# A float32 decoder trunk with an S5 layer: four GLU weight blocks unsplit, the second scan ahead of the splits, and the S5 preparation in four column groups

## The chip, the cores and the metric

The kernel runs on one core of a Trainium2 chip. The metric is device time of one execution in microseconds (us), the median of several runs. PE is the matrix engine (TensorE), PEld its weight loads, DVE the vector engine, ACT the scalar engine, POOL GpSimd, SP the engine that issues the transfers.

## The reference

Two layers of a residual trunk over 256 positions of width 2048, all in float32. Layer 0 is stick-breaking attention beside gated linear attention; layer 1 is an S5 state-space mixer with a GLU. Each is followed by a SwiGLU network (inner width 5632). What the change touches is layer 1 (left out below: `bb` is B scaled by (lb - 1) / lam, and the states s follow from a scan over the positions, s at l = lb times s at l - 1, plus bu at l):

```python
def s5_mixer(h, lam_re, lam_im, log_step, b_re, b_im, c_re, c_im, d_skip, w_glu):
    u = h.reshape(b_, L, 128, 16)                      # 128 groups of 16 channels
    dt = jnp.exp(log_step)[:, None]
    mag, ang = jnp.exp(dt * lam_re), dt * lam_im       # 64 complex states a group
    lb_re, lb_im = mag * jnp.cos(ang), mag * jnp.sin(ang)
    ...
    bu_re = jnp.einsum('blgh,gph->blgp', u, bb_re)
    bu_im = jnp.einsum('blgh,gph->blgp', u, bb_im)
    ...
    y = (jnp.einsum('ghp,blgp->blgh', c_re, s_re)
         - jnp.einsum('ghp,blgp->blgh', c_im, s_im) + d_skip * u)
    y = jax.nn.gelu(y.reshape(b_, L, D_MODEL), approximate=False)
    val, gate = jnp.split(y @ w_glu, 2, axis=-1)       # w_glu: 2048 x 4096
    return val * jax.nn.sigmoid(gate)
```

## The kernel before

**Split products.** A large product is made of three cheap ones. `Stream` loads the weights in chunks of 512 rows by 512 columns (1 MB, three buffers `wraw`), in the order of a plan. `convert` splits half a chunk (a *unit*: 256 rows) into `whi`, rounded by ACT, and `wlo`, the rest, by DVE. The activations are split likewise into `xh` and `xl`. `products` (lines 190 to 192) then issues, for each 128 rows of weights and each half `tb` of the 256 positions, xh·whi, xh·wlo and xl·whi, so that a unit takes 12 matmuls of 512 columns. `linear` walks the units of one block of 512 output columns after the other. `pairwise` walks two blocks together, four units of rows at a time, and calls a hook ahead of a unit whose number is in its table.

**Background work.** `s5_prep` is a generator that `pump` advances between units while layer 0's SwiGLU network (`ffn(0, ...)`) runs. From the S5 parameters it makes tables on DVE and ACT, writes them to DRAM, reads them back, and multiplies them in small float32 products on PE (line 1221): for each of 16 `k`, two halves, each of 2 `ri` by 2 `q` matmuls with 32 output rows. They go to 32-column groups of the array, two groups in a half. A result is written out as `t_d`.

**Opening of layer 1.** The tail of the network's last block adds its output to the residual `h[0]` and `h[1]` (two halves of 128 positions; `close` updates four blocks of 512 columns of a half, `squares` sums their squares on ACT, `rstds` makes the reciprocal roots, `normed` scales). `hold` names the blocks of `h[0]` whose update is put off to the tail.

**S5 mixer (`layer1`).** The channels are in four groups G of four tiles. `stage_a` transposes the normed input (line 1374), `stage_v` and `stage_b` rearrange it into `U`, `stage_x` multiplies it by a table into `xt` (line 1398), `stage_t` transposes that (line 1407) and copies it into the state `X`. `scan(0)` covers G 0 and 1, `scan(1)` G 2 and 3: a `pairs(2)` over 15 chunks, 14 short steps that depend on one another, a `pairs(3)`, all on DVE; `steps(sc, n)` issues n of these 16. `within(G)` (line 1418) and `out(G)` (line 1470) form the output, which DVE transposes into `y` and ACT puts through Gelu. The first two GLU blocks are a `pairwise` of 16 units; the units 0 to 7 read G 0 and 1, the units 8 to 15 read G 2 and 3. `out(2)` and `out(3)` are issued by its hooks.

All engines run in the written order. Nearly all vector and scalar work is recorded at line 65, so that it is told apart by its tiles.

## Time and profile before

| | |
|---|---|
| median of 3 runs | 2222.76 us (2219.78 to 2223.53) |
| profiled execution | 2222.8 us |
| its span, first to last instruction | 2220.9 us |
| mean granted TensorE clock | 0.992 |
| PE busy | 2172.9 us, 98% of the span |
| DVE busy | 1380.1 us, 62% |
| ACT busy | 985.0 us, 44% |
| DMA | 457.44 MB, mean 206 GB/s |

The profile is of one execution. Its own time is 0.04 us above the median, and 1.9 us of it lie outside the span. Matmuls overlap at their ends, so that the distance between two starts, not the length of one, is what a matmul costs.

### The profile page before, as it was taken

The numbers are of one execution on the slowest core, as the hardware profiler recorded it, in microseconds if no ns is written. First come the engines' busy times: TensorE is split into PE (matmuls) and PEld (weight loads), VectorE is DVE, ScalarE is ACT, GpSimd is POOL, SyncE is SP. The second block draws the span as 40 slices with busy tenths as digits, with TensorE's granted clock in tenths as the row PEclk, the third lists the DMA queues.
The fourth block names the chain that finished last, engine by engine and source line by source line (L and its number), as shares of the span: only waits on it lengthen the run. The fifth ranks groups of instructions, "written<-read, shape, count | busy, mean of one in ns | idle before, by whom it ended". The sixth has DMA issues, their size and how long they took to land.

```text
span 2220.9 us, 27098 instructions
## 1 busy us (share of the span) xinstructions
PE 2172.9 (98%) x10704; PEld 1752.5 (79%) x10704; DVE 1380.1 (62%) x1917; ACT 985.0 (44%) x1242; POOL 7.1 (0%) x14
## 2 busy tenths in 40 slices
PE   8999999999999999999998699999999999999998
PEld 6888888788888887777776578878888888888886
DVE  4676645657779997895456875464544444444545
ACT  5444545464444444434344444464444444433433
POOL 0000000000000000000000000000000000000000
PEclk9999999999999999999999899999999999999999
DMA  7554554555687777898768846546555555555553
GB/s 228 170 180 153 166 174 152 190 193 174 224 250 245 236 238 243 275 284 264 242 203 330 334 155 212 182 171 208 174 190 180 196 178 197 175 193 186 189 171 133
DMA packets 266351, 457.44 MB, mean 206 GB/s; under 512 B 23248, under 2 KB 68576, under 8 KB 265328
## 3 DMA queue, kind: packets, MB, share of 16 engines
q1 hardware_dynamic: 265504, 451.00, 61.3%
q0 software_dynamic: 720, 4.72, 0.5%
q8 instruction: 84, 1.38, 0.2%
q14 instruction: 43, 0.35, 0.0%
HBM read 425.26 MB, written 30.41 MB: 205 GB/s over the span
## 4 chain that ended last, share of the span: by engine, by line
PE 94%; DVE 3%; ACT 1%; DMA 0%; issue 0%; SPq 0%; DVEq 0%; ACTq 0%
PE lin L190 30%; PE lin L192 29%; PE lin L191 29%; PE big L465 1%; PE big L1221 1%; DVE wlo L65 1%; DVE X L65 1%; PE big L192 0%; PE big L792 0%; PE big L191 0%; PE big L190 0%; DVE h L65 0%; DVE xl L65 0%; ACT xh L65 0%; DMA wraw<-w_in 0%
## 5 line engine op out<-in xcount | busy, mean ns | idle before, releaser
L65 DVE TENSOR_TENSOR wlo<-wraw,whi 128x1024 fp32r<-128x1024 f32 x713 | 864.8, 1234 | 563.4 <-ACT whi L65 563.0
L65 ACT CAST whi<-wraw 128x1024 fp32r<-128x1024 f32 x713 | 731.4, 1049 | 654.7 <-PE lin L192 578.1
L190 PE MATMUL lin<-whi,xh 128*128 128x512 f32 x2016 | 804.6, 399 | 11.0 <-ACT xh L65 11.0
L191 PE MATMUL lin<-wlo,xh 128*128 128x512 f32 x2016 | 798.1, 396 | 2.2 <-DVE wlo L65 2.1
L192 PE MATMUL lin<-whi,xl 128*128 128x512 f32 x2016 | 798.1, 396 | 1.2 <-DVE xl L65 1.2
L190 PEld LDWEIGHTS lin<-whi,xh 128*128 128x128 f32 x2016 | 380.8, 189 | 102.8 <-ACT xh L65 12.2
L192 PEld LDWEIGHTS lin<-whi,xl 128*128 128x128 f32 x2016 | 380.6, 189 | 92.5 <-DVE xl L65 3.7
L191 PEld LDWEIGHTS lin<-wlo,xh 128*128 128x128 f32 x2016 | 381.0, 189 | 91.5 <-DVE wlo L65 5.6
L190 PE MATMUL lin<-whi,ah 128*128 128x512 f32 x680 | 270.2, 397 | 0.0
L192 PE MATMUL lin<-whi,al 128*128 128x512 f32 x680 | 268.4, 395 | 0.0
L191 PE MATMUL lin<-wlo,ah 128*128 128x512 f32 x680 | 268.3, 394 | 0.0
L190 PEld LDWEIGHTS lin<-whi,ah 128*128 128x128 f32 x680 | 127.8, 188 | 32.2 <-issue 2.6
L192 PEld LDWEIGHTS lin<-whi,al 128*128 128x128 f32 x680 | 127.7, 188 | 30.7
L191 PEld LDWEIGHTS lin<-wlo,ah 128*128 128x128 f32 x680 | 127.8, 188 | 29.7
L65 DVE SCALAR_TENSOR_TENSOR a<-lin,rs,a 128x512 f32<-128x512 f32 x44 | 31.0, 747 | 60.0 <-PE lin L192 60.0
L65 ACT ACTIVATE a<-lin,rs 128x512 f32<-128x512 f32 x44 | 27.9, 684 | 90.0 <-PE lin L192 90.0
L65 ACT ACTIVATE junk<-yg 128x512 f32<-128x512 f32 x24 | 15.2, 632 | 74.2 <-DVE yg L65 74.2
L65 ACT CAST ah<-big 128x1024 fp32r<-128x1024 f32 x22 | 22.3, 1015 | 55.4 <-PE big L465 55.4
L65 DVE TENSOR_TENSOR ed<-C,lam 128x288 f32<-128x288 f32 x64 | 43.1, 673 | 4.4 <-DMA C<-s_c_re 4.4
L65 DVE TENSOR_TENSOR yg<-lin,yg 128x512 f32<-128x512 f32 x30 | 20.0, 689 | 41.3 <-PE lin L192 41.3
L65 DVE TENSOR_TENSOR tt<-C,lam 128x288 f32<-128x288 f32 x64 | 43.3, 676 | 0.5 <-DMA C<-s_c_im 0.5
L65 DVE TENSOR_TENSOR tt<-lam,B 128x256 f32<-128x256 f32 x56 | 37.5, 670 | 8.9 <-DMA win_d<-win 8.9
(316 smaller groups left out, 1273.3 us busy)
## 6 DMA issues: line engine op xcount, KB each, us to landing
wraw<-w_ffn_in SPq DMA_DIRECT2D x176, 1024.0 KB, 5.0
wraw<-w_ffn_out SPq DMA_DIRECT2D x88, 1024.0 KB, 5.3
wraw<-w_in SPq DMA_DIRECT2D x47, 1024.0 KB, 5.0
wraw<-w_glu SPq DMA_DIRECT2D x32, 1024.0 KB, 5.4
wraw<-w_out SPq DMA_DIRECT2D x16, 1024.0 KB, 5.0
e_d<-ed SPq DMA_DIRECT2D x64, 144.0 KB, 4.4
et<-e_d SPq DMA_DIRECT2D x32, 288.0 KB, 4.6
win_d<-win SPq DMA_DIRECT2D x32, 256.0 KB, 8.3
```

The source lines that it names most:

```text
L65: return f(*a, **k)
L190: mm(ps, lhsT=xh, rhs=hi[:, kk, :], start=(k == 0), stop=False)
L191: mm(ps, lhsT=xh, rhs=lo[:, kk, :], start=False, stop=False)
L192: mm(ps, lhsT=xl, rhs=hi[:, kk, :], start=False, stop=(k == len(acts) - 1))
L465: nc.tensor.transpose(p[:, tb, i, :], a[:, tb, i * 128:(i + 1) * 128], self.ident)
L1221: nc.tensor.matmul(p[r:r + 32, :], lhsT=bt[:, q, ri, :], rhs=et[:, q, ri, 0:128], start=(ri == 0), stop=(ri == 1))
```

## The change

1. The four chunks of the GLU weights that the units 0 to 7 use are not split: `convert` hands out the raw half chunk, and `products` multiplies it by the unsplit `y` in float32, one matmul in place of three. `reload` counts such a chunk's buffer as free when its units have been used.
2. Around the scans: `stage_t(0)` and `stage_t(1)` stand ahead of `stage_b(2)`; half of their copies into `X` go to DVE. The four splits behind the first scan are gone, and the second scan is issued as 1, 3 and 12 steps around `out(0)` and `out(1)`, ahead of all splits. `out(2)` and `out(3)` stand ahead of unit 5. The splits of `y` (`high`, `low`) come at the units 5, 9 and 11.
3. Opening of layer 1: no block of `h[0]` is held back; the update, squares and norms of the two halves are interleaved.
4. `s5_prep`: B, C and the powers `lam` are laid out (on the host and in SBUF) so that the operands of most DVE operations are contiguous. The products of a `k` are one group of 2 `ri` by 4 `q` matmuls over four column groups. The table for it is fetched once for a `k`, into one buffer, after the products of the `k` before.

```diff
@@ Stream
+        self.raw, self.free = set(), 0
@@ Stream.convert
+        if c in self.raw:
+            self.split.append((raw, None))
+            return
         hi, lo = to or (self.part("whi", f"whi{u}"), self.part("wlo", f"wlo{u}"))
@@ Stream.reload
-            room = len(self.split) // 2 + self.raw_bufs
+            while (self.used if self.free in self.raw else len(self.split)) >= 2 * self.free + 2:
+                self.free += 1
+            room = self.free + self.raw_bufs
@@ products
+        if lo is None:
+            for kk in range(2):
+                k = 2 * u + kk
+                mm(ps, lhsT=self.whole[k][:, tb * 128:(tb + 1) * 128], rhs=hi[:, kk, :], start=(k == 0), stop=(k == len(acts) - 1))
+            return
@@ plan
+        ws.raw = set(range(self.glu_chunk, self.glu_chunk + 4))
@@ ffn, build
-                    evac, close, yg, gb, ss = self.post(layer, 3, final, (2,) if final else (2, 3))
+                    evac, close, yg, gb, ss = self.post(layer, 3, final, (2,) if final else ())
-            self.ffn(0, False, lambda: self.squares(0, (0, 1)), enter)
+            self.ffn(0, False, lambda: self.squares(0), enter)
@@ s5_prep
-        lam = sp.tile([128, 2, 64, 9], F32, tag="lam", name="lam", bufs=1)
+        lam = sp.tile([128, 2, 9, 64], F32, tag="lam", name="lam", bufs=1)
-        B = st("B").rearrange("g (r p h) -> g r p h", r=2, p=64)
+        B = st("B").rearrange("g (r h p) -> g r h p", r=2, h=16)
-        C = st("C").rearrange("g (r h p) -> g r h p", r=2, h=16)
+        C = st("C").rearrange("g (r p h) -> g r p h", r=2, p=64)
...
         for k in range(16):
-            for half in range(2):
-                et, bt = nxt
-                if 2 * k + half < 31:
-                    nxt = fetch(2 * k + half + 1)
-                yield
-                yield
-                p = self.pbig([128, 128])
-                for ri in range(2):
-                    for q in range(2):
-                        r = 64 * half + 32 * q
-                        nc.tensor.matmul(p[r:r + 32, :], lhsT=bt[:, q, ri, :], rhs=et[:, q, ri, 0:128], start=(ri == 0), stop=(ri == 1))
-                yield
-                pr = slice(64 * half, 64 * half + 64)
-                nc.scalar.copy(kp[pr, k % 2, 112:240], p[pr])
+            for _ in range(5):
+                yield
+            p = self.pbig([128, 128])
+            for ri in range(2):
+                for q in range(4):
+                    nc.tensor.matmul(p[32 * q:32 * q + 32, :], lhsT=bt[:, q, ri, :], rhs=et[:, q, ri, 0:128], start=(ri == 0), stop=(ri == 1))
+            yield
+            nc.scalar.copy(kp[:, k % 2, 112:240], p)
+            if k < 15:
+                fetch(k + 1)
@@ layer1, opening
-        self.squares(0, (2, 3))
-        r0, ry = self.rstds([self.hss[0], self.yss[1]])
-        self.close(1, ry)
+        (ry,) = self.rstds([self.yss[1]])
+        self.close(1, ry, (0, 1))
+        self.squares(1, (0, 1))
+        (r0,) = self.rstds([self.hss[0]], between=lambda: self.close(1, ry, (2,)))
+        self.squares(1, (2,))
         normed(0, 0, r0, nc.scalar)
+        self.close(1, ry, (3,))
+        normed(0, 2, r0, nc.vector)
+        self.squares(1, (3,))
         normed(0, 1, r0, nc.scalar)
-        self.squares(1)
-        normed(0, 2, r0, nc.vector)
-        normed(0, 3, r0, nc.vector)
-        (r1,) = self.rstds([self.hss[1]])
+        (r1,) = self.rstds([self.hss[1]], between=lambda: normed(0, 3, r0, nc.vector))
@@ layer1, stage_t and its place
-                nc.scalar.copy(dst, p[:, ri].rearrange("p k (q c) -> p k q c", q=4))
+                copy = nc.vector.tensor_copy if ri and G < 2 else nc.scalar.copy
+                copy(dst, p[:, ri].rearrange("p k (q c) -> p k q c", q=4))
@@ layer1, out and the hooks of the GLU
-        ws.limit = len(ws.loaded)
-        ws.fill(ws.used + 4)
         steps(s1, 1)
-        out(0, 2)
-        out(1, 2)
-        ws.limit = None
...
-        hooks = {n: more(2) for n in range(7)}
-        hooks[7] = more(30, 2)
-        hooks[10] = more(0, 3)
-        self.glu(s5, hooks)
+        out(0)
+        steps(s1, 3)
+        out(1)
+        steps(s1, 12)
+        def last():
+            out(2)
+            out(3)
+            high(2, 3)
+            low(2, 3)
+        def first(G):
+            def f():
+                high(G)
+                low(G)
+            return f
+        self.glu(s5, {5: last, 9: first(0), 11: first(1)})
```

**PE in `s5_prep`.** The instructions of PE around the first of these products, before. `big` is the PSUM tile that they write, `et` the tile that holds the fetched tables, `lin` the tile of the network's block, and x4 counts matmuls of the code.

```order
L191 MATMUL lin_6198<-wlo_6200,xh_91 128x512
L192 MATMUL lin_6198<-whi_6199,xl_92 128x512
L1221 MATMUL big_6281<-et_6217 32x128 x4
L190 MATMUL lin_6198<-whi_6223,xh_91 128x512
L191 MATMUL lin_6198<-wlo_6224,xh_91 128x512
```

And now:

```order
L204 MATMUL lin_6198<-wlo_6264,xh_91 128x512
L205 MATMUL lin_6198<-whi_6263,xl_92 128x512
L1229 MATMUL big_6346<-et_6217 32x128 x8
L203 MATMUL lin_6198<-whi_6285,xh_91 128x512
L204 MATMUL lin_6198<-wlo_6286,xh_91 128x512
```

Thirty-two insertions of four matmuls between the network's products have become sixteen of eight.

**PE and DVE where the GLU begins.** PE before, from the end of `out(0)` (`e` and `ring` hold its tables) to the first unit of the GLU:

```order
L1470 MATMUL lin_9606<-ring_9009,X 32x128 x16
L1470 MATMUL lin_9639<-ring_9010,X 32x128 x16
L1470 MATMUL lin_9639<-e_9554,X 32x128 x16
L1470 MATMUL lin_9639<-e_9556,X 32x128 x16
L1470 MATMUL lin_9639<-e_9705,X 32x128 x16
L190 MATMUL lin_10001<-whi_9799,xh_9796 128x512
L191 MATMUL lin_10001<-wlo_9800,xh_9796 128x512
L192 MATMUL lin_10001<-whi_9799,xl_9797 128x512
```

PE now, from the same place to `out(2)`:

```order
L1485 MATMUL lin_9542<-ring_8945,X 32x128 x16
L1485 MATMUL lin_9575<-ring_8946,X 32x128 x16
L1485 MATMUL lin_9575<-e_9490,X 32x128 x16
L1485 MATMUL lin_9575<-e_9492,X 32x128 x16
L1485 MATMUL lin_9575<-e_9641,X 32x128 x16
L198 MATMUL lin_9969<-wraw_9484,y_9811 128x512 x8
L198 MATMUL lin_9970<-wraw_9486,y_9811 128x512 x8
L198 MATMUL lin_9969<-wraw_9488,y_9901 128x512 x4
L1485 MATMUL big_9608<-e_8954,X 32x128 x2
```

DVE before, from the end of the first scan (`pt` and `X`) to the transposes of the first `y`:

```order
L65 TENSOR_TENSOR X<-X,pt_9790 128x15x2x32
L65 TENSOR_TENSOR wlo_9800<-wraw_9548,whi_9799 128x1024
L65 TENSOR_TENSOR wlo_9804<-wraw_9548,whi_9803 128x1024
L65 TENSOR_TENSOR wlo_9808<-wraw_9550,whi_9807 128x1024
L65 TENSOR_TENSOR wlo_9812<-wraw_9550,whi_9811 128x1024
L65 TENSOR_TENSOR pt_9816<-lam_4140,X 128x960
L65 TENSOR_TENSOR pt_9815<-lam_4140,X 128x960
L65 TENSOR_TENSOR X<-X,pt_9816 128x15x2x32
L65 TENSOR_TENSOR X<-X,pt_9815 128x15x2x32
L65 STREAM_TRANSPOSE y_9891<-lin_9606 128x8x32 x4
```

DVE now:

```order
L65 TENSOR_TENSOR X<-X,pt_9726 128x15x2x32
L65 TENSOR_TENSOR pt_9736<-lam_4140,X 128x960
L65 TENSOR_TENSOR pt_9735<-lam_4140,X 128x960
L65 TENSOR_TENSOR X<-X,pt_9736 128x15x2x32
L65 TENSOR_TENSOR X<-X,pt_9735 128x15x2x32
L65 STREAM_TRANSPOSE y_9811<-lin_9542 128x8x32 x4
```

The four splits between the scans are gone, and the units 0 to 4 of the GLU need nothing but `y` and raw weights, with `out(2)` behind them.

**ACT in the opening of layer 1.** Before, from the last square of the network's output (`yg` into `ss`) to the norms; `junk` with `hss` are squares of `h`, `rs` the roots:

```order
L65 ACTIVATE junk_9197,ss_4569<-yg_4567 128x512
L65 ACTIVATE junk_9202,hss_4570<-h_71 128x512
L65 ACTIVATE junk_9204,hss_4570<-h_71 128x512
L65 ACTIVATE rs_9206<-rs_9206,eps 128x1
L65 ACTIVATE rs_9207<-rs_9207,eps 128x1
L65 ACTIVATE yg_4566<-h_71,rs_9206 128x512 x2
L65 ACTIVATE junk_9228,hss_4571<-h_72 128x512
L65 ACTIVATE junk_9230,hss_4571<-h_72 128x512
L65 ACTIVATE junk_9232,hss_4571<-h_72 128x512
L65 ACTIVATE junk_9234,hss_4571<-h_72 128x512
L65 ACTIVATE rs_9238<-rs_9238,eps 128x1
L65 ACTIVATE yg_4567<-h_72,rs_9238 128x512 x2
```

And now:

```order
L65 ACTIVATE junk_9139,ss_4569<-yg_4567 128x512
L65 ACTIVATE rs_9142<-rs_9142,eps 128x1
L65 ACTIVATE junk_9152,hss_4571<-h_72 128x512
L65 ACTIVATE junk_9154,hss_4571<-h_72 128x512
L65 ACTIVATE rs_9156<-rs_9156,eps 128x1
L65 ACTIVATE junk_9165,hss_4571<-h_72 128x512
L65 ACTIVATE yg_4566<-h_71,rs_9156 128x512
L65 ACTIVATE junk_9170,hss_4571<-h_72 128x512
L65 ACTIVATE yg_4566<-h_71,rs_9156 128x512
L65 ACTIVATE rs_9173<-rs_9173,eps 128x1
L65 ACTIVATE yg_4567<-h_72,rs_9173 128x512 x2
```

Both norms of `h[0]` by ACT (`yg_4566`) now stand behind three and four squares of `h[1]`, and ahead of the root for `h[1]`.

## Rows read from the trace of the kernel before

**Rows 1.** The page of the profiled execution: busy time of the engines, and the chain of work that ended last by engine.

```profile
PE 2172.9 (98%) x10704; PEld 1752.5 (79%) x10704; DVE 1380.1 (62%) x1917; ACT 985.0 (44%) x1242; POOL 7.1 (0%) x14
...
PE 94%; DVE 3%; ACT 1%; DMA 0%; issue 0%; SPq 0%; DVEq 0%; ACTq 0%
```

**Rows 2.** Waits of PE over the whole span, longest in total first: what waited, for whom, us in total, times, the longest.

```profile
PE lin L190 <- ACT xh L65: 11.0, 2, 7.9
PE big L1374 <- ACT yg L65: 5.3, 1, 5.3
...
PE lin L1470 <- DVE X L65: 3.4, 1, 3.4
```

**Rows 3.** [...] The first three rows lie around the S5 mixer; the last is the stretch in which `s5_prep` multiplies.

```profile
1212.05:1218.57 6.52, 5.09 (x22) 4.29 (x23) 4.77 (x14) 4.97 (x12) 0.00 (x0) 0.50 1.03 420
...
1255.20:1269.35 14.15, 6.03 (x256) 5.83 (x257) 14.08 (x17) 1.30 (x3) 0.00 (x0) 0.75 0.82 288
1269.35:1323.54 54.19, 53.83 (x449) 42.12 (x449) 42.77 (x91) 24.24 (x31) 0.53 (x1) 0.94 0.53 188
832.00:1181.00 349.00, 349.00 (x1676) 272.96 (x1675) 238.81 (x324) 142.75 (x176) 0.00 (x0) 1.00 0.80 250
```

**Rows 4.** Timeline of PE around the first small products of `s5_prep` (line 1221): start us, us, engine, line, operation, output and inputs, shapes, count.

```profile
831.91 0.40 PE L192 MATMUL lin<-whi,xl 128*128 128x512 f32 x1
832.24 0.63 PE L1221 MATMUL big<-et 128*32 128x128 f32 x8
832.80 0.50 PE L190 MATMUL lin<-whi,xh 128*128 128x512 f32 x1
833.14 0.39 PE L191 MATMUL lin<-wlo,xh 128*128 128x512 f32 x1
```

**Rows 5.** All instructions of line 1221: ns min/median/max, first and last start, shapes.

```profile
L1221 PE MATMUL big<-et x256: 272/273/297, 832.2 to 1175.6; 128*32 128x128 f32 x128
```

**Rows 6.** Timeline of PE: full float32 products in the attention of layer 0 (line 905, 256 columns; each product of the code leaves two records).

```profile
240.45 0.59 PE L905 MATMUL big<-sqT,skT 128*128 128x256 f32 x2
240.88 0.38 PE L906 MATMUL big<-sqT,skT 128*128 128x128 f32 x2
```

**Rows 7.** Timeline of PE in `within` of the S5 mixer (line 1418): float32 products with 32 output rows that go round all four column groups; 16 records each.

```profile
1245.43 0.65 PE L1418 MATMUL lin<-t__9252,U 128*32 128x128 f32 x16
1245.89 0.62 PE L1418 MATMUL lin<-t__9254,U 128*32 128x128 f32 x16
```

**Rows 8.** Timeline of PE in the first two blocks of the GLU: the first products of the units numbered 2, 3 and 7 of 16, the 128 records of `out(2)` between units 6 and 7, and (last row) the first product behind the 16 units.

```profile
1278.40 0.40 PE L190 MATMUL lin<-whi,xh 128*128 128x512 f32 x1
...
1281.20 0.39 PE L190 MATMUL lin<-whi,xh 128*128 128x512 f32 x1
...
1292.45 1.81 PE L1470 MATMUL big<-e,X 64*32 64x128 f32 x90
...
1294.87 0.50 PE L190 MATMUL lin<-whi,xh 128*128 128x512 f32 x1
...
1323.54 0.39 PE L190 MATMUL lin<-whi,xh 128*128 128x512 f32 x1
```

**Rows 9.** Timeline of DVE from the end of layer 0 to the first transposes of the S5 input.

```profile
1209.86 0.16 DVE L65 TENSOR_REDUCE rs<-hss 128x1 f32<-128x4 f32 x1 [0.43 <-ACT junk L65]
...
1211.40 2.74 DVE L65 SCALAR_TENSOR_TENSOR h<-yg,rs,h 128x512 f32<-128x512 f32 x4
...
1215.52 0.16 DVE L65 TENSOR_REDUCE rs<-hss 128x1 f32<-128x4 f32 x1 [0.59 <-ACT junk L65]
...
1218.57 2.03 DVE L65 STREAM_TRANSPOSE v__9301<-big 128x256 f32<-128x256 f32 x4 [0.81 <-PE big L1374]
```

**Rows 10.** Timeline of ACT in the same stretch: the first of four squares of `h[1]` (each has a record that reads the sum behind it), and the norms of `h[1]`.

```profile
1212.52 0.62 ACT L65 ACTIVATE junk<-h 128x512 f32<-128x512 f32 x1
...
1216.88 1.33 ACT L65 ACTIVATE yg<-h,rs 128x512 f32<-128x512 f32 x2 [0.87 <-DVE rs L65]
```

**Rows 11.** Timeline of PE in the same stretch: transposes of the normed input (line 1374), four for each call of `stage_a`.

```profile
1214.59 1.97 PE L1374 MATMUL lin<-ident,yg 128*128 128x128 f32 x8 [0.57 <-DVE yg L65]
1217.42 1.97 PE L1374 MATMUL big<-ident,yg 128*128 128x128 f32 x8 [0.86 <-DVE yg L65]
```

**Rows 12.** Timeline of DVE: copy of the second `xt`, start of the first scan, its first and last short steps, the splits behind it, the transposes of the first `y`.

```profile
1229.38 1.42 DVE L65 COPY xt__9388<-big 128x256 f32<-128x256 f32 x4 [1.86 <-PE big L1398]
1235.15 1.16 DVE L65 TENSOR_TENSOR pt__9559<-lam,X 128x960 f32<-128x960 f32 x1 [4.35 <-ACT X L65]
...
1239.67 0.36 DVE L65 TENSOR_TENSOR sc<-lam,X 128x64 f32<-128x64 f32 x2
...
1250.80 2.23 DVE L65 TENSOR_TENSOR pt<-lam,X 128x960 f32<-128x960 f32 x2
...
1255.20 7.38 DVE L65 TENSOR_TENSOR wlo<-wraw,whi 128x1024 fp32r<-128x1024 f32 x4
...
1266.90 2.02 DVE L65 STREAM_TRANSPOSE y<-lin 128x256 f32<-128x256 f32 x4
```

**Rows 13.** Timeline of ACT: the four copies into `X` ahead of the scan.

```profile
1231.32 3.80 ACT L65 COPY X<-big 128x512 f32<-128x512 f32 x4
```

**Rows 14.** Timeline of PE: a gap in `stage_x(1)` (line 1398), and the first product of the GLU.

```profile
1228.72 0.62 PE L1398 MATMUL big<-ring,U 128*32 128x128 f32 x10 [1.64 <-issue]
...
1269.35 0.79 PE L190 MATMUL lin<-whi,xh 128*128 128x512 f32 x1 [7.89 <-ACT xh L65]
```

More of the change, by code (lines that the diff above doesn't have):

```diff
@@ L372, in update @@
                     nc.sync.dma_start(self.io["out"][0, tb * 128:(tb + 1) * 128, c], self.h[tb][:, c])
-            for nb in range(4):
+            for nb in blocks:
                 if tb == 0 and nb in hold:
@@ L1033, in s5_prep @@
         V.tensor_add(s1, s1, t)
-        L = [[lam[:, ri, :, mm] for mm in range(9)] for ri in range(2)]
+        L = [[lam[:, ri, mm] for mm in range(9)] for ri in range(2)]
         V.tensor_mul(L[0][1], mag, c1)
@@ L1183, in win @@
             for h0 in range(0, 16, 4):
-                b = [B[:, ri, :, h0:h0 + 4].rearrange("g p h -> g h p") for ri in range(2)]
+                b = [B[:, ri, h0:h0 + 4] for ri in range(2)]
                 for j in range(8):
@@ L1434, in layer1 @@
         stage_x(1)
+        stage_t(0)
+        stage_t(1)
         stage_b(2)
+        stage_b(3)
         self.e_load(3, e_slot(ring[0]))
@@ L1460, in layer1, with out @@
         nc.scalar.preload_act_table(AF.Gelu)
-        def out(G, n=0):
+        g = {}
+        self.whole = {}
+        def out(G):
             for kt in range(4 * G, 4 * G + 4):
@@ L1475, in out @@
                     self.e_load(kt + 8, self.e_at[kt])
-            us = range(2 * G, 2 * G + 2)
-            gs = []
-            ys = u4(f"y{G}").rearrange("p (a i x) -> p a i x", a=2, i=2)
-            for u in us:
-                y = ys[:, u % 2]
-                for i in range(2):
-                    nc.vector.transpose(y[:, i].rearrange("p (c j) -> p j c", j=8), Y[G][:, :, 2 * (u % 2) + i].rearrange("p e (j h) -> p j e h", j=8))
-                nc.scalar.activation(y, y, AF.Gelu)
-                nc.scalar.copy(self.xh[:, 2 * u:2 * u + 2], y)
-                gs.append(y)
@@ L1486, in out @@
-            steps(s1, n)
-            for u, g in zip(us, gs):
-                hi, lo = self.xh[:, 2 * u:2 * u + 2], self.xl[:, 2 * u:2 * u + 2]
-                nc.vector.tensor_sub(lo, g, hi.bitcast(F32))
-        ws.limit = len(ws.loaded)
-        ws.fill(ws.used + 4)
-        steps(s1, 1)
-        out(0, 2)
-        out(1, 2)
-        ws.limit = None
-        def more(n, *Gs):
+            g[G] = u4(f"y{G}").rearrange("p (k x) -> p k x", k=4)
+            for k in range(4):
+                y = g[G][:, k]
+                nc.vector.transpose(y.rearrange("p (c j) -> p j c", j=8), Y[G][:, :, k].rearrange("p e (j h) -> p j e h", j=8))
+                if k % 2:
+                    y = g[G][:, k - 1:k + 1]
+                    nc.scalar.activation(y, y, AF.Gelu)
+                self.whole[4 * G + k] = g[G][:, k]
@@ new lines, in high, with low @@
+        def high(*Gs):
+            for G in Gs:
+                for k in (0, 2):
+                    nc.scalar.copy(self.xh[:, 4 * G + k:4 * G + k + 2], g[G][:, k:k + 2])
+        def low(*Gs):
+            for G in Gs:
+                for k in (0, 2):
+                    s = slice(4 * G + k, 4 * G + k + 2)
+                    nc.vector.tensor_sub(self.xl[:, s], g[G][:, k:k + 2], self.xh[:, s].bitcast(F32))
+        steps(s1, 1)
+        out(0)
+        steps(s1, 3)
+        out(1)
+        steps(s1, 12)
```

57 lines of the change are left out of this document (26 added, 31 removed).

## The prediction

> **What bounds the kernel now.** I read the page first. PE is busy for 98% of the span, and PE makes 94% of the chain that ended last, DVE 3%, ACT 1% [rows 1]. So the time is PE's work plus the few places where PE stands still, and an edit counts only if it takes work off PE or shortens such a place. The waits of PE say where these are: 11.0 us for `xh` (7.9 of it once), 5.3 us for the normed input, 3.4 us for the state `X` [rows 2]. The windows put a stage to each. In the 349 us in which `s5_prep` multiplies, PE is busy throughout and DVE for 239 us, so only PE's own work counts there; around the mixer the clock is 0.50 to 0.94 and DVE is busy for 14.08 of 14.15 us just ahead of the GLU [rows 3]. There DVE is the bound. The timelines then give prices.
>
> **Part 1, the products of `s5_prep`.** Between two split matmuls PE needs 0.232 us (2.80 us for the 12 of a unit [rows 8]). At an insertion, from the split matmul ahead of it to the second one behind it, the starts lie 1.23 us apart (831.91 to 833.14), 0.77 us more than two such steps; the eight records alone are 0.56 of it [rows 4]. There are 256 records, so 32 insertions [rows 5], 24.5 us of PE. The change leaves 16 insertions of 16 records each. Products of the same shape that go round four column groups take 0.46 us for 16 records [rows 7]. If I put that in the place of what 8 records on two groups occupy, an insertion stays near 0.77; I take 0.80, as twice as many records wait to be started: 12.8 us. **Saved: 11.7 us.** Bounds: with the array as for two groups, 16 records need 0.56 twice, an insertion 1.33, and 24.5 - 21.3 = 3.2 is saved; with nothing added but the 0.46, an insertion is 0.67 and 13.8 is saved. I stay near the upper end since rows 7 are the same shape, 128x32 by 128 columns.
>
> [...]
>
> The other edits of `s5_prep` I cost at nothing. Contiguous operands make DVE faster in a stretch where PE never waits for it (110 us of DVE free in 349 [rows 3]). The table now has one buffer, fetched about six pumps (17 us by 2.80 a unit) ahead of its products; were it late, PE would stop in its order behind it.
>
> **Part 2, opening of layer 1.** Before, the joint root begins at 1209.86, the updates of `h[1]` at 1211.40, four squares take 1212.52 to 1215.52 on ACT (0.75 each), and the norms of `h[1]` start 1.36 later at 1216.88; the first `stage_v` starts at 1218.57 [rows 9, 10]. Now only one root stands ahead of the updates: 1209.9 + 1.36 = 1211.25. But ACT, in order, then does two squares (to 1213.6), the root of `h[0]`, a third square, one norm, a fourth square and the second norm (0.66 each [rows 10]): it ends near 1217.0, and the root for `h[1]` follows: norms at 1218.1. PE needs that second norm for its second group of transposes. Four groups of four at 0.98 us (eight in 1.97 [rows 11], the clock at 0.50 [rows 3]) then lie ahead of the first `stage_v`: 1217.05 + 3.9 = 1221.0. So I expect this opening to be about **2.5 us later**; were PE at full clock, 0.6. At best, with ACT never behind, the last update, its square and the root end at 1211.25 + 2.74 + 0.75 + 1.36 = 1216.1 and it gains 0.8.
>
> **Part 3, to the start of the scan.** Before, DVE waited 1.86 us for PE at the second `xt` copy, behind a gap of 1.64 us on PE that nothing in the profile explains [rows 12, 14], and then 4.35 us for four copies into `X` on ACT, 3.80 us [rows 12, 13]. Now `stage_t(1)` follows the `xt` copy at once, and its two copies run on ACT and DVE beside each other: about 1.0 for the transposes, 0.95 for a copy, 2.1 in all. DVE was ready for that copy at 1227.52. With the opening 2.5 late and the gap swallowed by that lateness the scan starts at 1230.0 + 1.4 + 2.1 = 1233.5; with the gap pushed along, 1235.2. I take 1234.0, against 1235.15.
>
> **Part 4, scan to GLU.** Unchanged on DVE: the first scan, 20.05 us (1235.15 to 1255.20; a short step is 11.13/14 = 0.795, a `pairs` 4.5). Before, four splits and a `pairs` took 11.70 us (1255.20 to 1266.90) ahead of the transposes of `y`; with Gelu and a rounding behind them PE began at 1269.35 [rows 12, 14]. Now `pairs` (4.5) and the transposes of `y` (2.0) follow, and Gelu of the first half of `y` lies beside the second half's transposes: the GLU starts at 1234.0 + 20.05 + 6.5 = 1260.5, **8.8 us earlier**.
>
> A raw unit is four float32 products. One of 256 columns takes 0.43 us in two records [rows 6], so one of 512 takes 0.86, and a unit 3.44 instead of 2.80: 8 units cost 5.1 us more. Five of them end at 1277.7. DVE meanwhile has three short steps (2.4), the second `y` (2.0), eleven short steps (8.75) and a `pairs` (4.5): 1278.2. So `out(2)` starts then, both outs take 2 x 2.42 [rows 8] and some, to 1283.3; three raw units to 1293.6; eight split units and 0.8 of small gaps to 1316.8. Before, this point is 1323.54: 6.7 us earlier. The clock is left: 0.94 over 54.19 us was 3.3 us lost before [rows 3]. The new stretch has a shorter stop ahead of it; I charge half, 1.6. **Saved: 5.1 us**, opening and scan included. Bounds: 10 with the opening no later and no slow clock, 0 with the gap kept, the opening 3 us late and the slow clock long.
>
> The weights need not be waited for: three raw chunks are loaded ahead as now, the fourth when unit 1 ends (about 1267), 19 us ahead of its use.
>
> **Sum.** 2222.8 (the profiled execution, which is also the median) - 11.7 - 5.1 = **2206.0 us**.
>
> **The rivals.**
> - *Two groups' worth only.* The sixteen records overlap no better than eight did, or each costs a time of its own to be started: part 1 saves 3 to 5. Against it stands the rate of [rows 7]. 2222.8 - 4 - 5.1 = 2213.7. [...]
> - *The S5 stretch gives nothing.* Opening later, gap kept, slow clock: the raw units' 5.1 us eat the earlier start. 2222.8 - 11.7 = 2211.1. For it: the ACT order, rows 10 and 11.
> - *The S5 stretch gives all.* No lateness, no gap, full clock: 2222.8 - 11.7 - 10 = 2201.1.
> - *The raw units run at the lower clock (slower than before).* A unit would be 6.88; all eight add 27.5 less the 1.6 already charged, 2206 + 25.9 = 2231.9. It decides from about five slow units (16.8/3.44). Against it, four records of rows 7 side by side take 0.115 us for 128 columns, the rate of the full products in rows 6 (0.215 for 256), and that with little else than float32 on PE; and before, the slow clock lasted about 6.5 us of the GLU's 54.19 (0.06 of it at half [rows 3]).
> - *The edits to `s5_prep` do nothing*, since PE waits for the next table or a split instead: 2222.8 - 5.1 = 2217.7. Against it: PE is busy all 349 us [rows 3], so nothing there is late enough now to be seen.
>
> **How the numbers follow.** Forecast (2203.5 to 2208.5) 0.45; S5 gives all 0.17; S5 gives nothing 0.18; two groups 0.09; `s5_prep` nothing 0.05; slow raw units 0.06. The range takes in all of these but the last two and some of the far ends: 2200 to 2214. Within 0.2% is 2218.3 to 2227.2, about what a measurement of this kernel can tell from no change. Faster 0.92, same 0.03, slower 0.05.
>
> **What the profile will show.** PE in `s5_prep`: 16 insertions, each 1.2 to 1.3 us between the same two starts as above; over 1.7 would mean no overlap. The first `stage_v` 9 to 10.5 us after the first update of `h[1]` where it was 7.2; this step is the one I trust least. The first raw product 26 to 27 us after the scan's start where it was 34.2. Starts of raw records 0.43 us apart; 0.85 would be the slow clock. `out(2)` behind unit 4 with a wait for `X` below 2 us. The prediction is wrong if the raw units run slow, or if PE waits ahead of the new insertions.

## Result, and the profile after the change

The changed kernel takes 2206.22 us (median of four runs, 2205.43 to 2207.28) against 2222.24 us (four runs, 2219.78 to 2223.53): a ratio of 0.993, 95% interval 0.9912 to 0.9947, so about 16 us faster. 2206.0 was predicted. The page of the profiled execution (2206.77 us, span 2205.0) has this row in the place of the first of [rows 1]: 12.9 us less of PE, 62 us less of DVE.

```profile
PE 2160.0 (98%) x10672; PEld 1738.9 (79%) x10672; DVE 1317.8 (60%) x1911; ACT 973.2 (44%) x1216; POOL 7.1 (0%) x14
```

The waits of PE (what waited, for whom, us in total, times, longest), which answer to [rows 2]:

```profile
PE big L1385 <- ACT yg L65: 8.9, 2, 8.7
...
PE lin L198 <- DVE sc L65: 1.5, 1, 1.5
PE big L1409 <- issue: 1.4, 1, 1.4
```

The 7.9 us ahead of the GLU have become 1.5 (`L198` is the raw product), the wait of the opening has grown, and waits called issue, of 0.6 to 1.4 us, are five now (two before, the longer one in [rows 14]).

Where the time went is read from landmarks on PE and DVE. Before, the last split product of layer 0 starts here (timeline of PE):

```profile
1206.37 0.40 PE L192 MATMUL big<-whi,al 128*128 128x512 f32 x1
```

| starts at, us | before | after | earlier by |
|---|---|---|---|
| last split product of layer 0 | 1206.37 | 1195.46 | 10.91 |
| first update of `h[1]` | 1211.40 | 1200.37 | 11.03 |
| first `stage_v` | 1218.57 | 1208.99 | 9.58 |
| first scan | 1235.15 | 1224.47 | 10.68 |
| first GLU product | 1269.35 | 1252.69 | 16.66 |
| first product behind the 16 units | 1323.54 | 1308.10 | 15.44 |
| end of the span | 2220.9 | 2205.0 | 15.9 |

The rows of the changed kernel behind this. PE at the first insertion of `s5_prep`, against [rows 4]: from the split product ahead (840.62) to the second one behind (841.85) it is 1.23 us, as it was, with 16 records in place of 8.

```profile
840.62 0.39 PE L205 MATMUL lin<-whi,xl 128*128 128x512 f32 x1
840.94 0.65 PE L1229 MATMUL big<-et 128*32 128x128 f32 x16
...
841.85 0.39 PE L204 MATMUL lin<-wlo,xh 128*128 128x512 f32 x1
```

DVE from the first updates of `h[1]` to the transposes of `y` for `out(2)`, against [rows 9, 12]:

```profile
1200.37 1.42 DVE L65 SCALAR_TENSOR_TENSOR h<-yg,rs,h 128x512 f32<-128x512 f32 x2
...
1208.99 2.03 DVE L65 STREAM_TRANSPOSE v__9237<-big 128x256 f32<-128x256 f32 x4 [1.26 <-PE big L1385]
...
1221.64 1.05 DVE L65 COPY X<-big 128x512 f32<-128x512 f32 x1 [0.67 <-ACT X L65]
1223.31 1.06 DVE L65 COPY X<-big 128x512 f32<-128x512 f32 x1 [0.62 <-ACT X L65]
1224.47 1.16 DVE L65 TENSOR_TENSOR pt__9495<-lam,X 128x960 f32<-128x960 f32 x1
...
1244.52 2.93 DVE L65 TENSOR_TENSOR pt<-lam,X 128x960 f32<-128x960 f32 x2
1247.38 2.34 DVE L65 TENSOR_TENSOR X<-X,pt 128x960 f32<-128x960 f32 x2
1249.65 2.78 DVE L65 STREAM_TRANSPOSE y<-lin 128x256 f32<-128x256 f32 x4
...
1254.51 2.03 DVE L65 STREAM_TRANSPOSE y<-lin 128x256 f32<-128x256 f32 x4
1265.04 2.23 DVE L65 TENSOR_TENSOR pt<-lam,X 128x960 f32<-128x960 f32 x2
...
1272.56 5.18 DVE L65 STREAM_TRANSPOSE y<-big 128x256 f32<-128x256 f32 x8 [3.04 <-PE big L1485]
```

ACT in the two copies into `X` that lie beside those of DVE, against [rows 13]:

```profile
1220.57 1.04 ACT L65 COPY X<-big 128x512 f32<-128x512 f32 x1 [5.42 <-PE big L1418]
1222.22 1.06 ACT L65 COPY X<-big 128x512 f32<-128x512 f32 x1 [0.61 <-PE big L1418]
```

PE from the end of layer 0 to the first product behind the 16 units of the GLU (L1385 is `stage_a`, L1409 `stage_x`, L1430 `within`, L1485 `out`), against [rows 8, 11, 14]:

```profile
1195.46 0.40 PE L205 MATMUL big<-whi,al 128*128 128x512 f32 x1
...
1208.35 1.04 PE L1385 MATMUL big<-ident,yg 128*128 128x128 f32 x8
...
1219.13 0.38 PE L1409 MATMUL big<-ring,U 128*32 128x128 f32 x2 [1.40 <-issue]
...
1228.20 1.29 PE L1409 MATMUL lin<-w,U 128*32 128x128 f32 x36 [1.20 <-issue]
...
1235.88 0.31 PE L1430 MATMUL lin<-t__9188,U 128*32 128x128 f32 x3 [0.77 <-issue]
...
1240.94 1.73 PE L1430 MATMUL big<-ring,U 128*32 128x128 f32 x55 [1.37 <-issue]
1244.75 2.24 PE L1485 MATMUL lin<-e,X 64*32 64x128 f32 x90 [2.07 <-DVE X L65]
...
1252.69 17.40 PE L198 MATMUL lin<-wraw,y 128*128 128x512 f32 x40 [1.52 <-DVE sc L65]
...
1275.39 10.57 PE L198 MATMUL lin<-wraw,y 128*128 128x512 f32 x24
1285.40 0.80 PE L203 MATMUL lin<-whi,xh 128*128 128x512 f32 x1
...
1308.10 0.40 PE L203 MATMUL lin<-whi,xh 128*128 128x512 f32 x1
```

And the clock, against [rows 3] (the stretch in us, its length, busy us of PE, PEld, DVE, ACT and POOL with their instructions in brackets, the granted clock as a share of full speed, the share of the DMA engines, GB/s; the opening, the two `out` ahead of the GLU, the first five raw units):

```profile
1195.86:1208.70 12.84, 3.96 (x20) 3.57 (x21) 9.22 (x30) 8.57 (x23) 0.20 (x1) 0.60 1.03 420
1244.75:1252.69 7.94, 6.29 (x256) 5.87 (x257) 7.91 (x11) 0.85 (x2) 0.00 (x0) 0.79 0.71 237
1252.69:1270.03 17.34, 17.34 (x40) 7.49 (x41) 15.88 (x62) 1.67 (x3) 0.00 (x0) 1.00 0.73 261
```

The start of the program can move by 1.5 us from one execution to the next (the last split product of layer 0 starts at 1195.46 us here and at 1193.97 in e9 below, whose work up to there is the same). So I compare the S5 stretch in times behind the last split product of layer 0, which for the changed kernel are 13.53 us for `stage_v`, 29.01 for the scan, 57.23 for the GLU.

### The profile page after: what moved, and what is told of

It reads as the page before. It is cut to its first block, busy times and chain, and to the rows that moved or that the text cites. A ratio compares the mean times of both kernels' runs of the same rounds, so it can differ in the third digit from the quotient of the medians.

```text
span 2205.0 us, 26937 instructions
## 1 busy us (share of the span) xinstructions
PE 2160.0 (98%) x10672; PEld 1738.9 (79%) x10672; DVE 1317.8 (60%) x1911; ACT 973.2 (44%) x1216; POOL 7.1 (0%) x14
## 3 DMA queue, kind: packets, MB, share of 16 engines
q8 instruction: 83, 1.36, 0.2%
## 4 chain that ended last, share of the span: by engine, by line
PE 94%; DVE 3%; ACT 1%; issue 0%; DMA 0%; SPq 0%; DVEq 0%; ACTq 0%
PE lin L203 29%; PE lin L205 29%; PE lin L204 29%; PE lin L198 1%; PE big L479 1%; DVE X L65 1%; PE big L806 0%; PE big L1229 0%; DVE h L65 0%; PE big L205 0%; PE big L204 0%; PE big L203 0%; ACT junk L65 0%; DVE wlo L65 0%; DVE xl L65 0%
## 5 line engine op out<-in xcount | busy, mean ns | idle before, releaser
L65 DVE TENSOR_TENSOR wlo<-wraw,whi 128x1024 fp32r<-128x1024 f32 x705 | 849.9, 1221 | 594.4 <-ACT whi L65 592.4
L203 PE MATMUL lin<-whi,xh 128*128 128x512 f32 x1984 | 789.8, 398 | 2.4 <-ACT xh L65 2.4
L204 PE MATMUL lin<-wlo,xh 128*128 128x512 f32 x1984 | 784.3, 395 | 2.2 <-DVE wlo L65 2.1
L205 PE MATMUL lin<-whi,xl 128*128 128x512 f32 x1984 | 784.2, 395 | 0.9 <-DVE xl L65 0.9
L203 PEld LDWEIGHTS lin<-whi,xh 128*128 128x128 f32 x1984 | 374.2, 189 | 90.6 <-ACT xh L65 3.0
L204 PEld LDWEIGHTS lin<-wlo,xh 128*128 128x128 f32 x1984 | 374.3, 189 | 90.0 <-DVE wlo L65 4.9
L65 DVE TENSOR_TENSOR al<-big,ah 128x1024 fp32r<-128x1024 f32 x22 | 26.9, 1223 | 17.0 <-ACT ah L65 17.0
L65 ACT ACTIVATE xh<-big,gT 128x128 fp32r<-128x128 f32 (+1 forms) x80 | 24.3, 395 | 22.1 <-PE big L337 16.9
L65 DVE SCALAR_TENSOR_TENSOR xl<-big,gT,xh 128x128 fp32r<-128x128 f32 (+1 forms) x80 | 24.5, 370 | 14.2 <-ACT xh L65 14.2
```

The lines of the kernel that those rows point to most:

```text
L65: return f(*a, **k)
L203: mm(ps, lhsT=xh, rhs=hi[:, kk, :], start=(k == 0), stop=False)
L204: mm(ps, lhsT=xh, rhs=lo[:, kk, :], start=False, stop=False)
L205: mm(ps, lhsT=xl, rhs=hi[:, kk, :], start=False, stop=(k == len(acts) - 1))
```

## The experiments

**The products alone, and with the layout (e1, e2).** e1 puts only this in the kernel before; e2 adds the layout of B, C and `lam`.

```diff
-                    for q in range(2):
-                        r = 64 * half + 32 * q
-                        nc.tensor.matmul(p[r:r + 32, :], lhsT=bt[:, q, ri, :], ...
+                    for q in range(4):
+                        nc.tensor.matmul(p[32 * q:32 * q + 32, :], lhsT=bt[:, q, ri, :], ...
```

> The kernel before with one edit alone: the products of the S5 preparation as 16 groups of 16 records over four column groups, the table fetched once for a k. Theory of the prediction: an insertion stays near 0.77 us though it holds twice the records, so 16 x 0.77 = 12.3 us of PE is saved, and 11 to 12.5 us of the time: 2210 to 2211 from 2222.2. Rival, records that overlap no better than on two groups: an insertion of 1.33, 3 to 5 us saved. [...]

> The kernel before with all edits of the S5 preparation: the products as in e1 and the contiguous layout of B, C and the powers. Theory: the layout only makes DVE quicker where PE waits for nothing, so it is worth nothing and the time is that of e1 within 1 us, while the DVE operations of the preparation become shorter. Rival: DVE was late somewhere in that stretch (a split that PE waits for), and this kernel is 1 us or more ahead of e1.

Measured: e1 2209.66 us, ratio 0.9944 (0.9931 to 0.9956), 12.6 us less than the 2222.22 of the kernel before on that chip; e2 2210.03 us, 0.9944 (0.9931 to 0.9958). The 16 insertions of e1 sum to 12.37 us by the measure of the prediction, the 32 of before to 24.49. The DVE operations on C and the powers (mean ns behind the bar), first in e1, then in e2:

```profile
L65 DVE TENSOR_TENSOR ed<-C,lam 128x288 f32<-128x288 f32 x64 | 42.8, 669 | 3.7 <-DMA C<-s_c_re 3.7
```

```profile
L65 DVE TENSOR_TENSOR ed<-C,lam 128x288 f32<-128x288 f32 x64 | 29.0, 453 | 4.7 <-DMA C<-s_c_re 4.7
```

So the column groups are worth 11 to 12 us, and the contiguous operands, with which these operations are a third quicker (DVE is busy for 438 us instead of 489 from 560 to 1195 us), are worth nothing that can be measured, since PE was busy throughout (635.00 of those 635.00 us in both).

Not all 12.6 us of e1 are due to the insertions. At its last split product (1195.27) 11.1 have arrived; another 1.4 come in the S5 stretch, whose code neither e1 nor e2 touches. The GLU of e2 starts 61.71 us behind the last split product (1195.33), that of e1 61.60, that of the kernel before 62.98:

```profile
1257.04 0.80 PE L190 MATMUL lin<-whi,xh 128*128 128x512 f32 x1 [5.92 <-ACT xh L65]
```

In both, `stage_v` stands at 11.74 us instead of 12.20, and the four splits beside `out` took 6.2 us instead of 7.38, with the granted clock at 0.60 instead of 0.72. These are single executions, so how often it happens is open. But against e2, the kernel with the same code ahead of the S5 stretch, the edits of the opening, the scans and the raw chunks save 3.8 us of the time (2210.03 to 2206.22) and 3.0 us up to the end of the 16 units. No run has the raw chunks without the other edits of that stretch.

**The old opening (e3).** `hold`, `squares` and the order in `layer1` as before the change.

> The changed kernel with the opening of layer 1 as it was before (two blocks of h[0] held back, one joint root, all squares of h[1] behind the norms of h[0]). In the traces the first stage_v starts 13.53 us behind the last split product after the change and 12.20 before it. Theory: the new opening costs its 1.3 us on the path to the scan and on to the end; with the old one the time is 1 to 1.5 us shorter, 2204.7 to 2205.2 from 2206.2. Rival: the gap on PE in stage_x (1.4 us, no cause shown) takes up the difference, and the time is within 0.4 us of the changed kernel's.

Measured: 2207.87 us (2204.69 to 2210.38), 0.9936 (0.9923 to 0.9948). In the trace `stage_v` stands 12.20 and the scan 27.79 us behind the last split product: the 1.2 us are there. At the GLU they are gone (57.14). DVE beside `out(0)` and `out(1)`:

```profile
1243.56 4.31 DVE L65 TENSOR_TENSOR pt<-lam,X 128x960 f32<-128x960 f32 x2
1247.80 2.86 DVE L65 TENSOR_TENSOR X<-X,pt 128x960 f32<-128x960 f32 x2
```

It took 7.2 us where the changed kernel took 5.3, and the windows (the two `out`, then the first raw products) say that the granted clock was 0.96 there instead of 0.79, and 0.55 afterwards:

```profile
1243.79:1252.86 9.07, 4.97 (x257) 4.56 (x257) 9.04 (x11) 0.86 (x2) 0.00 (x0) 0.96 0.71 235
1252.86:1259.70 6.84, 6.84 (x9) 2.88 (x10) 6.39 (x31) 1.66 (x3) 0.00 (x0) 0.55 0.96 365
```

Nine raw records in 6.84 us, 0.76 each instead of 0.43, cost about 3 us. The time is unsettled; the trace shows the opening's cost, and two things that can take it back.

**Two PSUM tiles for the copies into X (e4).**

```diff
-            p = tile_of(G)([128, 2, 4, 128])
+            ps = [self.pbig([128, 4, 128]), self.plin([128, 4, 128])]
```

> The changed kernel, with the transposed xt of groups 0 and 1 in two PSUM tiles, one for each half that is copied into X. In the changed kernel's trace the copies into X on ACT and DVE, meant to lie beside each other, follow one another (DVE idle 0.67 and 0.62 us for ACT's copy), and both read one PSUM tile. Theory: the order between readers of one tile is what serializes them; with a tile for each, DVE copies at once and the scan starts 0.9 to 1.1 us sooner behind the second xt copy (3.9 us instead of 4.92), the time 2205.2. Rival: the wait is due to X, which both write; then nothing changes.

Measured: 2208.04 us (2206.69 to 2208.43), 0.9936 (0.9923 to 0.9948). DVE:

```profile
1220.54 1.03 DVE L65 COPY X<-lin 128x512 f32<-128x512 f32 x1
1221.99 1.03 DVE L65 COPY X<-lin 128x512 f32<-128x512 f32 x1 [0.42 <-PE lin L1422]
1224.27 1.16 DVE L65 TENSOR_TENSOR pt__9497<-lam,X 128x960 f32<-128x960 f32 x1 [1.24 <-PE lin L1398]
```

The wait for ACT is gone though both still write `X`, so it was the two readers of one PSUM tile that the program put in order, and not `X`. But the scan now waits 1.24 us for `stage_b` (L1398), whose PSUM tile the new one occupied: from the last `xt` copy's end to the scan 3.65 us against 3.50. A wait was exchanged, nothing won.

**Three raw chunks (e5).** `ws.raw` has three chunks; `first(1)` stands at unit 4.

> The changed kernel with three raw chunks in place of four: the units 6 and 7 of the GLU are split, with the splits of y of group 1 ahead of out(2). A raw unit took 3.47 us in the changed kernel's trace (40 records in 17.34), a split one 2.80. Theory of the prediction: the price of a raw unit is PE time, and DVE, which waits 3.0 us for out(2) behind the scan, has the room for two splits of weights (2.4 us): the units 6 and 7 take 5.6 us instead of 6.9 and the end is 1.3 us sooner, 2204.9. Rival: the four chunks are needed since DVE is late without them: the transposes of y for out(2), or the splits for the units 8 on, come later, and the time is that of the changed kernel or longer.

Measured: 2207.58 us (2206.50 to 2210.38), 0.9938 (0.9924 to 0.9951). PE in `out(1)` and at unit 7:

```profile
1251.13 1.31 PE L1485 MATMUL lin<-e,X 64*32 64x128 f32 x55 [2.04 <-issue]
...
1283.93 0.50 PE L204 MATMUL lin<-wlo,xh 128*128 128x512 f32 x1 [0.76 <-DVE wlo L65]
```

The rival: unit 7 was converted only behind `out(2)`, and PE waited for it; a gap of 2.04 us ahead of the GLU, which the changed kernel has not, came on top. The price of a raw unit is not tested by this.

**The first y ahead (e6).**

```diff
-        steps(s1, 1)
+        next(s1); next(s1)
         out(0)
+        next(s1); next(s1)
```

> The changed kernel with the transposes of the first y moved ahead of the second half of the pairs that open the second scan, and out(2), out(3) at unit 6 instead of 5. In the changed kernel these four pair operations and four transposes take 8.05 us (2.93, 2.34, 2.78) where they take 6.6 (2.23, 2.34, 2.03) when PE is not in out(0), out(1), and the GLU starts 28.2 us behind the scan's start where 26.5 were predicted. Theory: that DVE chain sets the GLU's start; with 2.34 of it moved behind the transposes the GLU starts 1.3 to 1.6 us sooner (PE's out(0), out(1) themselves end about 6.6 us behind the scan) and the end with it: 2204.7. Rival: PE's out(0), out(1) already end too late for that; under 0.5 us.

Measured: 2205.75 us (2205.50 to 2205.98), 0.9927 (0.9915 to 0.994). The GLU starts 26.8 us behind the scan's start, 1.4 sooner, as the theory says. PE in `out(3)`:

```profile
1275.45 0.44 PE L1485 MATMUL big<-ring,X 64*32 64x128 f32 x5 [1.53 <-issue]
```

The gap here grew from 0.56 to 1.53 us, so that little of it reached the end.

**What the gaps are (e7).** 64 records of PE ahead of everything.

```diff
+                    for j in range(16):
+                        nc.tensor.matmul(p[0:32, :], lhsT=self.ident[:, 0:32], rhs=self.ident, ...)
```

> The changed kernel with 64 more records of PE at the very start of the program, where PE waits about 5 us for its first input. The gaps of 0.6 to 1.4 us on PE that the profile calls issue stand 126 recorded matmuls apart in the changed kernel (1219.13, 1228.20, 1235.88, 1240.94), which with their weight loads is 252 instructions, and the DMA page has a queue of kind instruction with 83 packets, 1.36 MB: 16 KB each. Theory: these gaps are PE waiting for the next 16 KB of its own instructions, so they stand at fixed counts of instructions; 64 records ahead move each of them 64 records back in the program: the one in stage_x(1) no longer stands two records ahead of its end but some 66, between stage_x(0) and stage_x(1). Rival: they come with a place or a load of the DMA queues; then the gap stays two records ahead of the end of stage_x(1). The time within 1.5 us of the changed kernel by either.

Measured: 2207.02 us (four runs, 2206.81 to 2207.17), 0.9933 (0.9919 to 0.9947). PE in the two `stage_x`, and at the one gap that is left:

```profile
1215.35 3.70 PE L1414 MATMUL big<-ring,U 128*32 128x128 f32 x128
...
1223.82 3.70 PE L1414 MATMUL lin<-w,U 128*32 128x128 f32 x128 [0.27 <-ACT U L65]
...
1236.83 0.31 PE L1435 MATMUL big<-t__9230,U 128*32 128x128 f32 x4 [2.01 <-issue]
```

The gap in `within` stood ahead of its 202nd recorded product and now stands ahead of its 138th: 64 records back, as the theory of instructions has it and the rival has not. The gap of `stage_x(1)` did not show between the two stages, as I had expected, but not at all; the place to which it moved lies soon behind a wait of PE (0.38 us at 1214.36), and that instructions arrived in such a wait is my reading, which no run shows. The scan starts 27.90 us behind the last split product, 1.1 sooner, though the opening was 0.6 later.

**What slows DVE beside out (e8, e9).** e8 reads other weights from X; e9 keeps the product and spreads X for all that read or write it.

```diff
-   lhsT=X[pr, 0:32, ri, 4 * kt + q]
+   lhsT=X[pr, 8 * ri + 2 * (kt % 4) + q // 2, q % 2, 32 * (G // 2):32 * (G // 2) + 32]        (e8)
-   X = s5.tile([128, 4224], ...).rearrange("p (c r g) -> p c r g", c=33, r=2)
+   X = s5.tile([128, 4356], ...).rearrange("p (c x) -> p c x", c=33)[:, :, 0:128]...          (e9)
```

> The changed kernel with other weights in out: 32 neighbouring elements of X instead of 32 that lie 512 bytes apart (the product of the states is then another one, all else is computed as before). Theory: the strided reads of X by PE's weight loads are what slows DVE beside out(0) and out(1); with neighbouring elements the four pair operations take 4.6 us there (5.3 in the changed kernel, 7.2 in e3 with PE at its full clock) and the GLU starts about 1 us sooner. Rival: any such run of small products slows DVE, whatever it reads, and they take over 5.2 us as before; a second rival, the table transfers issued in out, gives the same.

> The changed kernel with the state X laid out in steps of 528 bytes from one position to the next instead of 512 (four unused elements behind each), all work the same. In e8, where PE's weights were neighbouring elements, DVE's pair operations and transposes beside out took 2.22, 2.35, 2.04 and 2.03 us, in the changed kernel 2.93, 2.34, 2.78 and 2.6. Theory: it is the step of 512 bytes that makes the weight loads hinder DVE; with 528 DVE takes what it took in e8, the first raw product stands 26.7 us behind the scan's start (28.2 in the changed kernel), and the time is 1 to 1.5 us shorter. Rival: any reading that is not of neighbours hinders as much; then DVE takes as long as before and the time stays.

Measured: e8 2205.31 us (two runs), 0.9925 (0.9907 to 0.9944); e9 2206.34 us (2203.93 to 2206.91), 0.9928 (0.9915 to 0.994). DVE beside `out(0)` and `out(1)` in e9, the same to 0.03 us as in e8:

```profile
1242.99 2.22 DVE L65 TENSOR_TENSOR pt<-lam,X 128x960 f32<-128x960 f32 x2
1245.12 2.35 DVE L65 TENSOR_TENSOR X<-X,pt 128x960 f32<-128x960 f32 x2
1247.38 2.07 DVE L65 STREAM_TRANSPOSE y<-lin 128x256 f32<-128x256 f32 x4
```

These are the times that DVE takes beside the raw products (2.23 at 1265.04, 2.03 at 1254.51 in the changed kernel). The GLU starts 27.0 us behind the scan's start, now behind PE's own `out(1)`. The granted clock beside `out` was alike (0.74 in e8, 0.75 in e9, 0.73 in the changed kernel). So it was the step of 512 bytes between the weights, nothing else of `out`, that slowed DVE here. In the profiled execution the S5 stretch gains 1.3 us up to the GLU; the median of the runs does not show it.

**A filler in the opening (e10), and all together (e11, e12).** e10 is e3 with 64 records that nobody reads behind the last split product. e11 is e10 with e9 and e6. e12 is e11 with three raw chunks, the splits of the units 6 and 7 ahead of `out(2)`.

```diff
+        v0 = self.pbig([128, 4, 256])
+        for i in range(17):
+            nc.tensor.matmul(v0[0:32, i % 4, 0:128], lhsT=self.ident[:, 0:32], rhs=self.ident, ...)
+        for i in range(30):
+            nc.tensor.transpose(v0[:, i % 4, 0:128], self.ident, self.ident)
...
-        self.glu(s5, {5: last, 9: first(0), 11: first(1)})
+        self.glu(s5, {5: first(1), 6: last, 9: first(3), 11: first(0)})      (e12)
```

> The kernel of e3 (the changed kernel with the old opening) with 64 records of PE that nobody reads, 34 small products and 30 transposes, where PE waits 5.3 us behind the last split product of layer 0. Theory on the clock: the granted clock is 0.5 in the opening because PE stands still there; with this filler it stays at 1.0, eight transposes take 1.04 us instead of 1.97, and the first stage_v starts 11.3 to 11.7 us behind the last split product (12.20 in e3). Theory on the instructions: 64 records more ahead of stage_x put its gap behind a wait as in e7, which takes 1.5 us off the way to the scan. Together the scan starts 25.5 to 26.5 us behind the last split product instead of 27.8. Rivals: the filler holds PE up when the first norm is ready (stage_v no earlier than 12.2), or the gap returns in another place ahead of the scan.

> The three edits that worked, joined: the old opening with the filler of e10, the state in steps of 528 bytes of e9, and the order of e6 (first y ahead of the second half of the pairs, out(2) and out(3) at unit 6). Theory: the scan starts 25.5 us behind the last split product as in e10; beside out DVE takes its unhindered times, so that PE's out(0) and out(1) themselves, 5.5 to 6.7 us by the clock, set the start of the GLU, 51 to 52.5 us behind the last split product (53.8 in e10, 57.2 in the changed kernel); out(2) waits for nothing. The time is 1.5 to 2.5 us below e10's 2203.4: 2201 to 2202. Rival: what is gained ahead of the GLU comes back as a wait of out(2) for the second scan, or as a longer instruction gap there, and it stays within 0.5 us of e10.

> e11 with three raw chunks, mended where e5 failed: the splits for both units 6 and 7 stand ahead of out(2), and of the splits of y only those of group 2 behind it. Theory: two split units in place of raw ones save 1.3 us of PE (3.47 against 2.80 us each), and DVE is now in time for them: 1.0 to 1.3 us below e11. Rival: the splits for unit 8 come 1 us late or more, and nothing is gained.

Measured: e10 2203.36 us (2202.95 to 2203.70), 0.9916 (0.9903 to 0.993). `stage_v` stands 11.74 and the scan 25.51 us behind the last split product, and the clock (window of the opening) is full. PE:

```profile
1194.36:1206.10 11.74, 10.09 (x88) 9.33 (x87) 9.41 (x31) 8.96 (x23) 0.20 (x1) 1.00 1.03 419
```

```profile
1201.85 1.04 PE L1388 MATMUL big<-ident,yg 128*128 128x128 f32 x8
```

The filler does two things, and only one of them is shown to pay. `stage_v` at 11.74 us was reached in e1 and e2 without it. From `stage_v` to the scan e10 takes 13.77 us and e7, whose 64 records stand far ahead of the opening, 13.80, where e3 takes 15.59 and the changed kernel 15.48: most of these 1.7 to 1.8 us is the gap in `stage_x(1)` (1.53 and 1.40 us), which is gone in e10 and e7.

e11: 2204.83 us (2203.55 to 2207.17), 0.9929 (0.9917 to 0.9941). The GLU starts 52.24 us behind the last split product, as expected, but the rival took it back in `out(3)`:

```profile
1274.67 0.94 PE L1488 MATMUL big<-e,X 64*32 64x128 f32 x41 [3.29 <-issue]
```

So e11 saves 16.0 us against the kernel before on its chip where e10 saves 18.8, and the 2201 to 2202 expected were missed. The profiled execution, the fastest of e11, is level with that of e10 at the end of the 16 units (DVE reads the first result 110.0 and 109.9 us behind the last split product); what its slower executions lose is in no trace.

e12: 2199.75 us (four runs, 2199.39 to 2200.18) against 2220.85 for the kernel before on that chip: 0.9905 (0.9889 to 0.992). It beats both kernels, the changed one by 5 to 6 us (21.1 us saved against the kernel before, each on its own chip, where the changed one saves 16.0). The gap at the same place:

```profile
1271.68 0.94 PE L1488 MATMUL big<-e,X 64*32 64x128 f32 x41 [1.12 <-issue]
```

From the GLU's start to the first DVE operation on its result e12 takes 54.8 us, e11 57.8: 2.2 of the 3.0 are the gap, which leaves 0.8 for the two units where 1.3 was expected. The other 2 us between the two medians no trace shows.

## Why the prediction was right, and where its steps were not

**The number.** The forecast took 16.8 us off the 2222.8 of one execution; the four runs of the kernel before have 2222.24 as their median, and 16.0 are saved. That 2206.22 lies within 0.3 us of 2206.0 is luck: part 1 came out larger than said and the S5 stretch smaller.

**Part 1 held.** 12.1 us were saved at the insertions (11.7 predicted): an insertion costs 0.77, not even the 0.80. The 16 records occupy 0.57 us, nearly what 8 did (0.56); the 0.46 of [rows 7] did not come, and put in for the 0.56 it would have given 0.67, not the 0.77 that the prediction names. e1 shows part 1 alone. Up to the end of layer 0, 10.9 us arrive; some 0.8 go in small steps of PE that I did not trace, the rest in the start of the program. In e1 and e2 too 16 records took 0.57 us, 36 ns each. The edits costed at nothing cost nothing (e2).

**Part 2 charged too much for the clock.** The opening is 1.33 us later, not 2.5, and the sign named for it (9 to 10.5 us from the first update of `h[1]` to `stage_v`) was missed with 8.62. The roots and updates came as worked out (the first update 0.12 sooner, 0.15 said), the second norm of `h[0]` ended 0.3 sooner than said, the norms of `h[1]` began 0.88 later (1.2 said). What failed is the term of the transposes, 3.9 us at half clock: 3.1 were needed, as the clock came back among them (granted 0.50 from 1199.00 to 1208.00 us, 1.00 from 1208.35 to 1209.00), and eight took 1.04 instead of 1.97. This changes from one execution to the next. In e4, e5 and e7, which have the same opening, the eight took 1.91, and `stage_v` stands 14.1 us behind the last split product, 1.9 later than before.

**Part 3 failed in one step.** The gap was pushed along, which I had left open, and the two copies "on ACT and DVE beside each other" came one behind the other (1.04, 1.05, 1.06, 1.06 us from 1220.57 on), as both read one PSUM tile; e4 shows that order and that it is not enough to lift it. From the end of the last `xt` copy to the scan 3.50 us passed where 2.1 were charged. In the time frame of before (10.91 later) the scan starts at 1235.4, where 1234.0 was taken and 1235.2 named for a gap that stays.

**Part 4 was right by errors that cancel.** The scan took its 20.05 us, a raw record 0.434 us, eight split units 22.7. But the term "`pairs` (4.5) and the transposes of `y` (2.0)" took 8.05 (the sum of its rows; 7.91 from the first start to the last end): DVE was hindered by PE's reads of X with a step of 512 bytes (e8, e9). It stood in [rows 12]: four splits in 7.38 us beside the same `out`, 1.85 each. So the GLU began 28.2 us behind the scan's start where 26 to 27 were named, at 1263.6 in the frame of before, 3.1 later than said. 0.9 came back up to the end of the 16 units (1319.0 there, 1316.8 said), and the 1.6 charged for the clock was not needed: the raw units ran at 1.00. What is left, 4.5 us there and 5.0 at the end of the program, is near the 5.1 predicted. The half microsecond between comes in the later GLU blocks, cause not looked for. And this is measured against the one trace of the kernel before: against e2 the same edits are worth 3.0 us there and 3.8 of the time, so part 4 promised too much.

**The rivals.** That S5 gives nothing did not come (3.8 us against e2), though two of its conditions did, the later opening and the gap. The slow raw units came too, but in e3, for 6.84 us, at a price of about 3; the forecast had not seen that DVE would be slowest where PE runs fastest beside it (7.2 us at a clock of 0.96 in e3, 5.3 at 0.79 in the changed kernel). Both forms of the first rival are refuted by e1 (12.1 us at the insertions); the 3 of its "3 to 5" is the bound of 3.2, and the 5 no run shows. The one that the edits of `s5_prep` do nothing is refuted by it too.

Left open: what sets the length of a gap, when the clock comes back in the opening, and why the medians of e4 and e9 do not follow their traces closely.

## What to carry to other kernels

Before costing an operation at its lone duration, look what the other engines read beside it: an old row that ran long next to the same neighbour (1.85 against 1.23 us) gives the price. A gain on a chain of engines is kept only if the next wait does not take it (of the 1.4 us of e6 a gap that grew from 0.56 to 1.53 us took 1.0); compare landmarks behind a common point, not totals. Work for PE that shortens nothing, put where it stood still, paid here by where the gaps of PE fell (1.7 to 1.8 us from `stage_v` to the scan in e10 and e7); that it also pays by the clock is not shown. And an edit is priced against the run that shares all other code (e2), since a stretch whose code is the same took 1.4 us less in another kernel's run.
